# Products of the up-projection and parts of the down-projection by turns in the blocks done in sevens

## The chip, the cores and the metric

The kernel runs on one core of a Trainium2 chip. The metric is the time of one execution on the device in microseconds (us): before the change 2946.87, the median of three runs from 2945.6 to 2947.86.

The core has a matrix engine (TensorE, PE in the rows; its weight loads are PEld), a vector engine (VectorE, DVE), a scalar engine (ScalarE, ACT) and a general one (GpSimd, POOL). Each works through its own instructions in the order in which the program wrote them, and waits at each for what that one needs. SP issues the transfers (DMA), in order too.

## The reference

One layer of a decoder over 2048 prompt tokens and 64 sample tokens. The mixer in its first half stays as it is; the change lies in the MLP behind it, with D_MODEL = 1024 and D_FF = 4096, all in float32:

```python
h1 = layer_norm(ALPHA * h + mix, ln1_g, ln1_b)
up = jnp.square(jax.nn.relu(jnp.einsum('btd,df->btf', h1, w_up)))
ff = jnp.einsum('btf,fd->btd', up, w_down)
h  = layer_norm(ALPHA * h1 + ff, ln2_g, ln2_b)
```

## The kernel before

Each float32 operand is split into a high part (ScalarE copies it to a rounded type: `uph`, `wdh`, `uh`, `xsh`, `xoh`) and a low part (VectorE subtracts: `upl`, `wdl`, `ul`, `xsl`, `xol`). A product of two such operands is three matmuls (`mm3`, line 1786): high by high, high by low, low by high.

The MLP (`mlp_phase`) takes the tokens in three blocks: five token tiles, then six, then six. Blocks 1 and 2 do the up-projection "in sevens" (`block`, line 2062): hidden features f and f+16, two halves of the inner dimension and two halves of the 768 tokens make a 2 by 2 scheme that needs seven products where the plain way needs eight. A **round** of the loop (`up(j)`, line 2069, j from 0 to 15) makes seven **products** (`seven`): each is 12 matmuls of 384 columns. They go into three PSUM banks of a ring of four ("pu"), here called y, x and d: products 1, 3, 5 and 7 add into y, 2 and 4 into x, 6 into d. Between them y and x are read out (`m1`, `m5`, `u2`, slices of the tile `mt`), so the next product on the same bank must wait for that read. `done` turns a sum into the squared ReLU: three instructions of ScalarE, then one of VectorE for the low part `ul`.

`down(bi, fs, tasks)` (line 1917) is the down-projection of the round before, for its two features. It has 12 **parts**: for each half of the output columns and each token tile, 6 matmuls of 512 columns into one of four banks ("pd"), then an addition by VectorE into the token tile's accumulator `acc`. In a round of before all seven products come first, then all 12 parts. A bank is used again four parts later, when its addition is done.

Weights are loaded two features at a time into a ring of four buffers (`raw`): `unit.load` for the up-projection of the next round, `load_down` for the down-projection. `unit.one` to `unit.seven` make and split the seven combinations into four `slots`; one to four were tasks within the parts, five to seven come behind the first three products. `split_down` splits the down weights into four `wslots`, two for each half of the output.

Between two blocks (`last_two`, line 2012) the last two rounds' parts run back to back, and among them the next block's rows are transposed by TensorE into the "pu" banks and combined (`enters`, line 1842): for each of three pairs of token tiles two sets of transposes (`rows`), the combining (`sums`: seven instructions of VectorE, eight of ScalarE, four of GpSimd) and a scaling of the accumulators by ScalarE (`scale`). One of these steps was taken behind every second part. Layer norms of finished blocks and of the rows to come stand in a list `later`; `step()` takes one of them, and stands behind some products and some parts. `finish` (line 2156) ends the last block and is left as it is.

What runs when is set by the order in which these calls are written: each engine gets its instructions in that order.

Of the kernel before, what the change touches and what calls it, by code (L numbers as in the profile page):

```python
# [8 lines left out]
F32 = mybir.dt.float32  # L9
F32R = mybir.dt.float32r  # L10
U8 = mybir.dt.uint8
AF = mybir.ActivationFunctionType
# [1661 lines left out]
def mlp_phase(ctx, tc, em, a, o, z, banks, sch):  # L1674
# [167 lines left out]
    def enters(bi):  # L1842
# [3 lines left out]
        out = []  # L1846
        for mi in range(3):
# [33 lines left out]
            out += [lambda r=rows: r(0), lambda r=rows: r(1), sums, scale]  # L1881
        return out
# [34 lines left out]
    def down(bi, fs, tasks, last=False, todo=()):  # L1917

        acc = accs[bi % 2]
        n = 0  # L1920
        for hf in range(2):
            for mi, (t0, mt) in enumerate(blocks[bi]):
                ps = bank("pd")
                partial(ps, mi, mt, fs, wslots[2 * hf:2 * hf + 2], True, True)
                s = slice(512 * hf, 512 * hf + 512)
                em.tt(acc[mi][0:mt, s], ps[0:mt], acc[mi][0:mt, s], OP.add)
                if todo and n % 2 == 0:
                    todo.pop(0)()
                for x in tasks.get(n, ()):
                    x()  # L1930
                if n % 4 == 0 and not todo:
                    step()
                n += 1
        if last:
            while todo:
                todo.pop(0)()
            lns = []
            for mi, (t0, mt) in enumerate(blocks[bi]):
                def put(t0=t0, mt=mt, t=acc[mi]):
                    em.dma(o["y"][t0:t0 + mt], t[0:mt])  # L1940

                lns.append(layer_norm(acc[mi], mt, put))
            for i in range(len(lns) + 2):
                for j in range(3):
                    if 0 <= i - j < len(lns):
                        later.append(lns[i - j][j])
# [65 lines left out]
    def last_two(bi, fs, gs):  # L2012

        todo = enters(bi + 1)
        n = len(blocks[bi])
        down(bi, fs, {n + 1: [lambda: split_down(gs, (0,))]}, todo=todo)
        down(bi, gs, {0: [lambda: split_down(gs, (1,))], 2: [unit.one], 4: [unit.two], 6: [unit.three], 8: [unit.four]}, last=True, todo=todo)
# [44 lines left out]
    def block(bi):  # L2062
# [6 lines left out]
        def up(j):  # L2069
# [11 lines left out]

            def done(c, f, c0):
                em.act(c, c, AF.Relu)
                squared(c, f, c0)
# [5 lines left out]
            em.act(m5, x, AF.Copy)  # L2090
            unit.six()
            step()
# [3 lines left out]
            if j:  # L2096
                split_down((j - 1, j + 15), (0, 1) if j == 15 else (0,))
            if j == 15:
                load_down(f, g)
            seven(x, "xs", 12, 3)  # L2100
            em.tt(u2, x, u2, OP.add)
            if j < 15:
                unit.load()
            done(u2, g, 0)
            seven(y, "xs", 8, 0)
            em.tt(m5, y, m5, OP.add)
            if 0 < j < 15:
                split_down((j - 1, j + 15), (1,))
            if j < 15:
                load_down(f, g)  # L2110
            if j == 15 and not end:
                unit.load()
            if not j:
                unit.one()
                unit.four()
            done(m5, g, 384)
            seven(d, "xo", 4, 1, True)
            em.tt(m1, d, m1, OP.add)
            if not j:
                unit.two()  # L2120
            done(m1, f, 0)
            if j == 15 and end:
                late(3, f, 0)
                late(0, f, 1)
                late(1, g, 0)
# [3 lines left out]
            if not j:  # L2129
                unit.three()  # L2130
# [3 lines left out]
            step()  # L2134

        for j in range(16):
            up(j)
            if 0 < j < 15:
                down(bi, (j - 1, j + 15), {2: [unit.one], 4: [unit.two], 6: [unit.three], 8: [unit.four]})
# [171 lines left out]
```

## Time and profile before

| | us |
|---|---|
| median of three runs | 2946.87 |
| the profiled execution | 2953.42 |
| its span, first to last instruction | 2951.3 |
| TensorE busy in the span | 2825.0 (96%) |
| VectorE busy | 1985.0 (67%) |
| ScalarE busy | 1208.6 (41%) |
| GpSimd busy | 511.9 (17%) |
| rounds of block 1, from the first product to the last | 500.28 |
| rounds of block 2 | 492.67 |
| way from block 0 to block 1, and from block 1 to block 2 | 46.08, 46.67 |

TensorE is busy nearly all the time, and its matmuls overlap in the records: each is longer than the distance from its start to the next one's start. What a row of matmuls costs is therefore read from starts. Idle time in the rows stands in brackets, with the instruction that ended it.

### The profile page before, as it was taken

How to read it: one execution, taken by the hardware profiler on the slowest of the kernel's cores; microseconds unless marked ns; L12 is line 12 of the kernel's file. 1: busy time of each engine (PE TensorE's matmuls, PEld its weight loads, DVE VectorE, ACT ScalarE, POOL GpSimd, SP SyncE). 2: the span in 40 equal slices, each digit the busy share in tenths (PEclk: the TensorE clock that was granted, in tenths of full speed). 3: DMA queues.
4: the chain of work that ended last, by engine and by line, in shares of the span. 5: the costliest groups of instructions: out<-in, count | busy, mean ns of one | idle time of the engine just before them, and what ended most of it. 6: DMA issues, size and time to landing. Idle time of an engine off the chain costs nothing.

```text
span 2951.3 us, 54436 instructions
## 1 busy us (share of the span) xinstructions
PE 2825.0 (96%) x21918; PEld 2448.9 (83%) x21918; DVE 1985.0 (67%) x3812; ACT 1208.6 (41%) x2576; POOL 511.9 (17%) x505
## 2 busy tenths in 40 slices
PE   8999999999999999898999999899999989999998
PEld 8988877777778778798988888778888877888887
DVE  5876757868787687845455665675677567666566
ACT  5445323443444335233333333534443454443443
POOL 4332111011011013337100000210001021100003
PEclk9999999999999999899999999999999999999999
DMA  7535444524343443457532222123211112221121
GB/s 269 199 106 200 141 144 126 173 95 145 107 158 116 123 143 103 133 167 242 177 114 84 81 79 79 58 90 114 81 63 58 58 72 79 85 80 58 58 85 59
DMA packets 173773, 339.41 MB, mean 115 GB/s; under 512 B 29776, under 2 KB 51536, under 8 KB 173520
## 3 DMA queue, kind: packets, MB, share of 16 engines
q1 hardware_dynamic: 173520, 335.93, 33.6%
q8 instruction: 172, 2.82, 0.4%
q14 instruction: 81, 0.66, 0.1%
HBM read 272.75 MB, written 63.11 MB: 114 GB/s over the span
## 4 chain that ended last, share of the span: by engine, by line
PE 59%; DVE 18%; issue 11%; ACT 8%; POOL 2%; DMA 2%; SPq 0%; DVEq 0%; POOLq 0%; ACTq 0%
PE bank L97 57%; ACT mt L112 2%; DVE rhsb L156 2%; DVE xt L156 2%; DVE mt L156 2%; POOL raw L156 2%; PE bank L108 2%; DVE wdl L156 1%; DVE xt L1005 1%; ACT uh L112 1%; DVE acc L160 1%; DVE ul L156 1%; ACT uph L112 1%; DVE acc L156 1%; DVE upl L156 1%
## 5 line engine op out<-in xcount | busy, mean ns | idle before, releaser
L97 PE MATMUL bank<-wdh,uh 128*128 128x512 f32 (+1 forms) x1064 | 421.1, 396 | 20.2 <-DVE acc L156 18.9
L156 DVE TENSOR_TENSOR acc<-bank,acc 128x512 f32<-128x512 f32 (+1 forms) x532 | 351.5, 684 | 102.9 <-PE bank L97 100.0
L97 PE MATMUL bank<-wdh,ul 128*128 128x512 f32 (+1 forms) x1064 | 417.0, 392 | 0.0
L97 PE MATMUL bank<-wdl,uh 128*128 128x512 f32 (+1 forms) x1064 | 416.9, 392 | 0.0
L97 PE MATMUL bank<-xh,wh 128*128 128x512 f32 (+1 forms) x1040 | 384.0, 369 | 11.3 <-ACT wh L112 8.1
L97 PE MATMUL bank<-xl,wh 128*128 128x512 f32 (+1 forms) x1040 | 380.5, 366 | 0.7 <-DVE xl L156 0.7
L97 PE MATMUL bank<-xh,wl 128*128 128x512 f32 (+1 forms) x1040 | 375.0, 367 | 0.9 <-POOL wl L156 0.8
L97 PE MATMUL bank<-xoh,uph 128*128 128x288 f32 (+1 forms) x896 | 283.0, 316 | 32.9 <-DVE mt L156 27.8
L156 DVE TENSOR_TENSOR upl<-raw,uph 128x512 fp32r<-128x512 f32 x292 | 201.4, 699 | 162.2 <-ACT uph L112 162.1
L97 PE MATMUL bank<-xoh,upl 128*128 128x288 f32 (+1 forms) x896 | 280.4, 313 | 0.0
L97 PE MATMUL bank<-xol,uph 128*128 128x288 f32 (+1 forms) x896 | 280.2, 313 | 0.0
L97 PEld LDWEIGHTS bank<-wdh,uh 128*128 128x128 f32 (+1 forms) x1064 | 197.4, 186 | 75.9 <-DVE acc L156 33.5
L112 ACT ACTIVATE uph<-raw 128x512 fp32r<-128x512 f32 x292 | 174.4, 623 | 205.7 <-DVE raw L156 182.4
L97 PE MATMUL bank<-wh,xh 128*128 128x256 f32 (+1 forms) x816 | 248.0, 304 | 7.9 <-DVE rs L160 7.9
L97 PE MATMUL bank<-wh,xl 128*128 128x256 f32 (+1 forms) x816 | 234.8, 288 | 3.8 <-DVE xl L156 3.8
L97 PEld LDWEIGHTS bank<-wdh,ul 128*128 128x128 f32 (+1 forms) x1064 | 197.1, 185 | 46.6 <-issue 0.2
L97 PE MATMUL bank<-wl,xh 128*128 128x256 f32 (+1 forms) x816 | 234.9, 288 | 0.0
L97 PEld LDWEIGHTS bank<-wdl,uh 128*128 128x128 f32 (+1 forms) x1064 | 197.6, 186 | 43.1 <-issue 0.2
L97 PEld LDWEIGHTS bank<-xh,wh 128*128 128x128 f32 x1040 | 197.5, 190 | 40.9 <-ACT wh L112 8.3
L156 POOL TENSOR_TENSOR raw<-raw 128x512 f32<-128x512 f32 x64 | 89.2, 1394 | 784.6 <-DVE raw L156 410.9
L97 PEld LDWEIGHTS bank<-xl,wh 128*128 128x128 f32 x1040 | 197.5, 190 | 29.6 <-issue 4.6
L97 PEld LDWEIGHTS bank<-xh,wl 128*128 128x128 f32 x1040 | 196.2, 190 | 29.4 <-issue 4.8
(250 smaller groups left out, 5768.9 us busy)
## 6 DMA issues: line engine op xcount, KB each, us to landing
raw<-in_wup SPq DMA_DIRECT2D x96, 512.0 KB, 3.6
raw<-in_wdown SPq DMA_DIRECT2D x96, 512.0 KB, 4.1
wh<-h_w SPq DMA_DIRECT2D x156, 256.0 KB, 2.6
wl<-l_w SPq DMA_DIRECT2D x156, 256.0 KB, 2.9
raww<-in_wout SPq DMA_DIRECT2D x64, 256.0 KB, 2.8
raww<-in_win SPq DMA_DIRECT2D x52, 256.0 KB, 3.3
h_w<-wh SPq DMA_DIRECT2D x52, 256.0 KB, 2.8
l_w<-wl SPq DMA_DIRECT2D x52, 256.0 KB, 2.4
```

Of the source, the lines that this page charges most:

```text
L97: self.nc.tensor.matmul(out, lhsT, rhs, start=start, stop=stop, skip_group_check=skip)
L108: self.nc.tensor.transpose(out, in_, ident)
L112: self.nc.scalar.activation(out, in_, func, **kw)
L156: (self.nc.vector if eng == DVE else self.nc.gpsimd).tensor_tensor(out, a, b, op=op)
L160: self.nc.vector.scalar_tensor_tensor(out, a, s, b, op0=op0, op1=op1)
L1005: nc.vector.transpose(out, in_)
```

## The change

Three things are written in another order; no instruction of the computation is added or left out.

First, in rounds 1 to 14 of blocks 1 and 2 the 12 parts no longer follow the seven products. `groups` makes a list of them, and `go()` issues two: behind products 2, 3, 4, 5, 6 and 7. Rounds 0 and 15 have no parts among their products, as before.

Second, what went with it: the low part `ul` of each `done` is put off (`lows`, `low()`) until the next product has been issued and its sum read; `split_down` is halved, the first output half behind product 5 of the round itself, the second behind product 2 of the next; `unit.one` to `unit.four` come behind products 5, 6, 6 and 7; `load_down` now comes ahead of `unit.load`, behind product 2, and `unit.load` behind product 3. So the two change places in the ring of four buffers. `step()` is called three times in a round, where it was two times, and three more in the parts.

Third, between blocks the steps of `enters` are taken one behind each of three parts in a row, then a pause of three or four parts, and all scalings at the end.

```diff
+        gap = [None] * (len(blocks[bi - 1]) - 2)
+        return [x for steps in out for x in steps + gap][:-len(gap)] + scales
...
+        return [lambda x=(hf, mi, mt): group(*x) for hf in range(2) for mi, (t0, mt) in enumerate(blocks[bi])]
...
+            parts = groups(bi, (j - 1, j + 15)) if 0 < j < 15 else []
+
+            def go():
+                for _ in range(2):
+                    if parts:
+                        parts.pop(0)()
+
+            lows = []
+
             def done(c, f, c0):
                 em.act(c, c, AF.Relu)
-                squared(c, f, c0)
+                em.act(c, c, AF.Square)
+                uh, ul = [t[:, c0:c0 + 384] for t in us[f]]
+                em.act(uh, c, AF.Copy)
+                lows.append(lambda: em.tt(ul, c, uh.bitcast(F32), OP.subtract))
...
             seven(x, "xs", 0, 1, True)
             em.act(m5, x, AF.Copy)
+            if j:
+                split_down((j - 1, j + 15), (1,))
+            load_down(f, g)
             unit.six()
+            go()
             step()
             seven(y, "xs", 4, 2)
             em.act(u2, y, AF.Copy)
             unit.seven()
-            if j:
-                split_down((j - 1, j + 15), (0, 1) if j == 15 else (0,))
-            if j == 15:
-                load_down(f, g)
+            if j < 15 or not end:
+                unit.load()
+            go()
             seven(x, "xs", 12, 3)
             em.tt(u2, x, u2, OP.add)
-            if j < 15:
-                unit.load()
             done(u2, g, 0)
+            go()
+            step()
             seven(y, "xs", 8, 0)
             em.tt(m5, y, m5, OP.add)
-            if 0 < j < 15:
-                split_down((j - 1, j + 15), (1,))
+            low()
             if j < 15:
-                load_down(f, g)
-            if j == 15 and not end:
-                unit.load()
-            if not j:
+                split_down((f, g), (0,))
                 unit.one()
-                unit.four()
             done(m5, g, 384)
+            go()
             seven(d, "xo", 4, 1, True)
             em.tt(m1, d, m1, OP.add)
-            if not j:
+            low()
+            if j < 15:
                 unit.two()
+                unit.four()
             done(m1, f, 0)
+            go()
+            step()
...
-            if 0 < j < 15:
-                down(bi, (j - 1, j + 15), {2: [unit.one], 4: [unit.two], 6: [unit.three], 8: [unit.four]})
```

On TensorE, in round 1 of block 1 behind product 2 (`xs`, `uph`, `upl` are a product's operands; `wdh`, `wdl`, `uh`, `ul` a part's; six rows like the added ones, into bank 63, stand just ahead):

```order
+L97 MATMUL bank_66<-wdh_15656,uh_15665 128x512
+L97 MATMUL bank_66<-wdl_15657,uh_15665 128x512
+L97 MATMUL bank_66<-wdh_15656,ul_15666 128x512
+L97 MATMUL bank_66<-wdh_15658,uh_15734 128x512
+L97 MATMUL bank_66<-wdl_15659,uh_15734 128x512
+L97 MATMUL bank_66<-wdh_15658,ul_15735 128x512
 L97 MATMUL bank_64<-xsh,uph_14569 128x384
 L97 MATMUL bank_64<-xsl,uph_14569 128x384
```

Two parts now stand between product 2 and product 3, which adds into y's bank (64). The same is so behind each later product of the round.

On VectorE, in a middle round of block 2, around product 5, whose sum is read by the row `mt<-bank_64,mt`. Before:

```order
L156 TENSOR_TENSOR mt<-bank_69,mt 128x384
L156 TENSOR_TENSOR ul_15941<-mt,uh_15940 128x384
L156 TENSOR_TENSOR mt<-bank_64,mt 128x384
L156 TENSOR_TENSOR wdl_15661<-raw_14688,wdh_15660 128x512
L156 TENSOR_TENSOR wdl_15663<-raw_14740,wdh_15662 128x512
L156 TENSOR_TENSOR ul_15941<-mt,uh_15940 128x384
L156 TENSOR_TENSOR mt<-bank_70,mt 128x384
```

Now:

```order
L156 TENSOR_TENSOR mt<-bank_69,mt 128x384
L156 TENSOR_TENSOR acc_4_14457<-bank_63,acc_4_14457 128x512
L156 TENSOR_TENSOR acc_5_15653<-bank_66,acc_5_15653 128x512
L156 TENSOR_TENSOR mt<-bank_64,mt 128x384
L156 TENSOR_TENSOR ul_15941<-mt,uh_15940 128x384
L156 TENSOR_TENSOR wdl_15657<-raw_15695,wdh_15656 128x512
L156 TENSOR_TENSOR wdl_15659<-raw_15697,wdh_15658 128x512
L156 TENSOR_TENSOR upl_14566<-raw_14688,uph_14565 128x512
L156 TENSOR_TENSOR raw_14688<-raw_14740,raw_14688 128x512
L156 TENSOR_TENSOR acc_0_14453<-bank_67,acc_0_14453 128x512
L156 TENSOR_TENSOR acc_1_14454<-bank_68,acc_1_14454 128x512
L156 TENSOR_TENSOR mt<-bank_70,mt 128x384
```

The read of product 5's sum has moved ahead of the `ul` that waits for ScalarE, and additions of parts (`acc`) stand between the reads of sums.

On VectorE, at the end of the way from block 0 to block 1, the third `sums` (the rows of `mt` and `xol`). Before:

```order
L156 TENSOR_TENSOR acc_3_14456<-bank_67,acc_3_14456 128x512
L156 TENSOR_TENSOR upl_14572<-raw_14740,uph_14571 128x512
L156 TENSOR_TENSOR acc_4_14457<-bank_68,acc_4_14457 64x512
L156 TENSOR_TENSOR mt<-bank_64,mt 128x512
L156 TENSOR_TENSOR mt<-mt,bank_69 128x512
L156 TENSOR_TENSOR mt<-bank_69,mt 128x512
L156 TENSOR_TENSOR xol<-bank_69,xoh 128x4x128
L156 TENSOR_TENSOR mt<-bank_65,mt 128x512
L156 TENSOR_TENSOR xol<-bank_64,xoh 128x4x128
L156 TENSOR_TENSOR xol<-bank_65,xoh 128x4x128
L156 TENSOR_TENSOR upl_14566<-raw_14740,uph_14565 128x512
```

Now:

```order
L156 TENSOR_TENSOR acc_4_14457<-bank_67,acc_4_14457 64x512
L156 TENSOR_TENSOR mt<-bank_64,mt 128x512
L156 TENSOR_TENSOR mt<-mt,bank_69 128x512
L156 TENSOR_TENSOR mt<-bank_69,mt 128x512
L156 TENSOR_TENSOR xol<-bank_69,xoh 128x4x128
L156 TENSOR_TENSOR mt<-bank_65,mt 128x512
L156 TENSOR_TENSOR xol<-bank_64,xoh 128x4x128
L156 TENSOR_TENSOR xol<-bank_65,xoh 128x4x128
L156 TENSOR_TENSOR upl_14568<-raw_14688,uph_14567 128x512
L156 TENSOR_TENSOR raw_14688<-raw_14740,raw_14688 128x512
L156 TENSOR_TENSOR acc_0_14453<-bank_68,acc_0_14453 128x512
```

The third `sums` stood behind the last part's addition; now five additions of parts, and the two instructions of `unit.two`, stand behind it.

## Rows read from the trace of the kernel before

**Rows 1.** The page, part 1: busy us, share, instructions.
```profile
span 2951.3 us, 54436 instructions
PE 2825.0 (96%) x21918; PEld 2448.9 (83%) x21918; DVE 1985.0 (67%) x3812; ACT 1208.6 (41%) x2576; POOL 511.9 (17%) x505
```

**Rows 2.** TensorE's waits, 1868.87 to 2908.49: us in total, times, longest.
```profile
PE bank L97 <- DVE mt L156: 27.8, 30, 1.9
PE bank L97 <- DVE acc L156: 13.7, 21, 3.1
```

**Rows 3.** Stretches: from:to, length, busy (instructions) PE PEld DVE ACT POOL, clock, DMA.
```profile
1868.87:2369.15 500.28, 479.00 (x2353) 426.83 (x2354) 332.17 (x534) 214.94 (x407) 54.95 (x55) 0.99 0.22 79
2415.82:2908.49 492.67, 471.87 (x2352) 423.63 (x2353) 317.27 (x513) 215.27 (x408) 51.08 (x46) 1.00 0.19 71
1822.79:1868.87 46.08, 36.37 (x170) 28.21 (x169) 31.17 (x50) 21.30 (x36) 13.88 (x12) 0.91 0.07 23
2369.15:2415.82 46.67, 40.60 (x194) 32.98 (x193) 32.07 (x52) 22.37 (x38) 13.93 (x12) 0.96 0.10 39
1868.87:1905.47 36.60, 33.84 (x168) 33.23 (x169) 22.83 (x38) 23.14 (x43) 9.66 (x9) 0.88 0.17 61
2603.02:2618.72 15.70, 15.01 (x85) 14.71 (x84) 7.28 (x13) 8.38 (x16) 1.30 (x1) 1.00 0.22 75
2618.72:2635.09 16.37, 16.37 (x73) 13.53 (x73) 12.34 (x20) 5.32 (x10) 1.30 (x1) 1.00 0.14 57
2171.43:2188.91 17.48, 16.98 (x74) 13.37 (x74) 14.41 (x22) 5.31 (x10) 1.30 (x1) 1.00 0.13 53
```

**Rows 4.** Timeline of TensorE, one round of block 2: start, length; products, then parts.
```profile
2603.02 0.34 PE L97 MATMUL bank<-xoh,uph 128*128 128x384 f32 x1
...
2605.11 0.34 PE L97 MATMUL bank<-xsh,uph 128*128 128x384 f32 x1
...
2607.23 0.34 PE L97 MATMUL bank<-xsh,uph 128*128 128x384 f32 x1
...
2618.72 0.39 PE L97 MATMUL bank<-wdh,uh 128*128 128x512 f32 x1
...
2620.12 0.39 PE L97 MATMUL bank<-wdh,uh 128*128 128x512 f32 x1
...
2621.49 0.39 PE L97 MATMUL bank<-wdh,uh 128*128 128x512 f32 x1
```

**Rows 5.** Timeline of the same round around the wait ahead of product 7.
```profile
2615.36 0.56 DVE L156 TENSOR_TENSOR ul<-mt,uh 128x384 fp32r<-128x384 f32 x1 [1.71 <-ACT uh L112]
...
2615.84 0.55 DVE L156 TENSOR_TENSOR mt<-bank,mt 128x384 f32<-128x384 f32 x1
...
2616.53 0.41 PE L97 MATMUL bank<-xoh,uph 128*128 128x384 f32 x1 [0.69 <-DVE mt L156]
```

**Rows 6.** VectorE by line and shape, one round, 2603.02 to 2635.09: count, busy, mean ns.
```profile
L156 DVE TENSOR_TENSOR acc<-bank,acc 128x512 f32<-128x512 f32 x12 | 7.9, 684 | 1.5 <-PE bank L97 1.3
L156 DVE TENSOR_TENSOR upl<-raw,uph 128x512 fp32r<-128x512 f32 x7 | 5.0, 710 | 6.0 <-ACT uph L112 6.0
```

**Rows 7.** Timeline of the way from block 0 to block 1, VectorE, then TensorE.
```profile
1832.24 0.67 DVE L156 TENSOR_TENSOR mt<-bank,mt 128x512 f32<-128x512 f32 x1
...
1837.89 1.29 DVE L156 TENSOR_TENSOR xol<-bank,xoh 128x512 fp32r<-128x512 f32 x2 [1.18 <-ACT xoh L112]
...
1857.56 0.80 PE L97 MATMUL bank<-wdh,uh 128*128 128x512 f32 x1 [3.23 <-DVE acc L156]
...
1868.87 0.69 PE L97 MATMUL bank<-xoh,uph 128*128 128x384 f32 x1 [4.57 <-DVE xol L156]
```

**Rows 8.** Timeline of TensorE, block 1, product 2 of round 1.
```profile
1890.14 0.44 PE L97 MATMUL bank<-xsh,uph 128*128 128x384 f32 x1 [1.82 <-ACT c L112]
```

**Rows 9.** Timeline of VectorE, block 1, the longest `ul`.
```profile
1885.41 1.65 DVE L156 TENSOR_TENSOR ul<-mt,uh 128x384 fp32r<-128x384 f32 x1
```

**Rows 10.** The page, part 6: DMA issues, KB each, us to landing.
```profile
raw<-in_wup SPq DMA_DIRECT2D x96, 512.0 KB, 3.6
```

More of the change, by code (lines that the diff above doesn't have):

```diff
@@ L1842, in enters @@
     def enters(bi):
-        out = []
+        out, scales = [], []
         for mi in range(3):
@@ L1879, in scale @@
                     em.act(t, t, AF.Copy, scale=ALPHA)
-            out += [lambda r=rows: r(0), lambda r=rows: r(1), sums, scale]
-        return out
+            out.append([lambda r=rows: r(0), lambda r=rows: r(1), sums])
+            scales.append(scale)
+        gap = [None] * (len(blocks[bi - 1]) - 2)
+        return [x for steps in out for x in steps + gap][:-len(gap)] + scales
     def rest():
@@ L1915, in partial, with groups @@
             mm3(ps[0:mt], uh[:, c0:c0 + mt], ul[:, c0:c0 + mt], wh, wl, first and i == 0, last and i == len(fs) - 1)
-    def down(bi, fs, tasks, last=False, todo=()):
+    def groups(bi, fs):
         acc = accs[bi % 2]
[L1920 to L1929, printed above, removed]
-                    x()
[L1931 to L1946, printed above, removed]
@@ new lines, in group, with down @@
+        def group(hf, mi, mt):
+            ps = bank("pd")
+            partial(ps, mi, mt, fs, wslots[2 * hf:2 * hf + 2], True, True)
+            t = acc[mi][0:mt, 512 * hf:512 * hf + 512]
+            em.tt(t, ps[0:mt], t, OP.add)
+        return [lambda x=(hf, mi, mt): group(*x) for hf in range(2) for mi, (t0, mt) in enumerate(blocks[bi])]
+    def down(bi, fs, tasks, todo=()):
+        for n, g in enumerate(groups(bi, fs)):
+            g()
+            if todo:
+                x = todo.pop(0)
+                if x is not None:
+                    x()
+            for x in tasks.get(n, ()):
+                x()
+            if n % 4 == 0 and not todo:
+                step()
@@ L1948, in next_rows, with last_norms, put @@
+    def last_norms(bi):
+        lns = []
+        for mi, (t0, mt) in enumerate(blocks[bi]):
+            def put(t0=t0, mt=mt, t=accs[bi % 2][mi]):
+                em.dma(o["y"][t0:t0 + mt], t[0:mt])
+            lns.append(layer_norm(accs[bi % 2][mi], mt, put))
+        for i in range(len(lns) + 2):
+            for j in range(3):
+                if 0 <= i - j < len(lns):
+                    later.append(lns[i - j][j])
     def next_rows(bi):
@@ L2016, in last_two @@
         down(bi, fs, {n + 1: [lambda: split_down(gs, (0,))]}, todo=todo)
-        down(bi, gs, {0: [lambda: split_down(gs, (1,))], 2: [unit.one], 4: [unit.two], 6: [unit.three], 8: [unit.four]}, last=True, todo=todo)
+        down(bi, gs, {0: [lambda: split_down(gs, (1,))], 2: [unit.one], 4: [unit.two], 6: [unit.three], 8: [unit.four]}, todo=todo)
+        while todo:
+            todo.pop(0)()
+        last_norms(bi)
     class Unit:
@@ L2128, in up @@
                 late(2, g, 1)
-            if not j:
+            low()
+            if j < 15:
                 unit.three()
@@ L2133, in up @@
             squared(c, f, 384)
-            step()
+            go()
         for j in range(16):
             up(j)
-            if 0 < j < 15:
-                down(bi, (j - 1, j + 15), {2: [unit.one], 4: [unit.two], 6: [unit.three], 8: [unit.four]})
             if not end:
```

4 lines of the change are left out of this document (added).

## The prediction

> **What bounds the kernel now.** The page first: TensorE is busy for 2825.0 of 2951.3 us, VectorE for 67%, ScalarE for 41% [rows 1]. So time can only go where TensorE idles or runs slowly. The rounds of blocks 1 and 2, which the change rewrites, are 500.28 + 492.67 = 992.95 us long [rows 3]; TensorE's waits there come next: 27.8 us in 30 waits for a `mt` of VectorE, 13.7 us in 21 waits for an `acc` [rows 2]. The reader is to see that both releasers are VectorE, though VectorE is busy for 7.28 + 12.34 = 19.62 of the 32.07 us of an ordinary round [rows 3]. It is not too slow, it does things in the wrong order.
>
> That shows in one round [rows 5]. Product 7 adds into y and must wait until VectorE has read product 5's sum (`mt`, at 2615.84). VectorE came to it late, because ahead of it in the queue stood the `ul` of the sum before, which idled 1.71 us for ScalarE's three instructions. TensorE had only product 6 to do meanwhile and idled 0.69. The waits for `acc` are in rounds with norms: there the parts take 17.48 instead of 16.37 [rows 3], since steps of norms stand between the additions, and a bank is wanted again four parts later.
>
> **What TensorE must do in a round.** From start to start [rows 4]: a product on `xo` takes 2605.11 - 2603.02 = 2.09, one on `xs` 2607.23 - 2605.11 = 2.12. Three and four of them make 6.27 + 8.48 = 14.75; the round of before took 15.70, so its wait with the slow restart behind it costs 0.95. The parts: the first behind the products takes 2620.12 - 2618.72 = 1.40, the second 1.37, and the ten others (16.37 - 2.77) / 10 = 1.36.
>
> **The change part by part.** *Turns.* Two parts stand behind each of products 2 to 7. A pair behind a product has been seen to take 1.40 + 1.37 = 2.77, so six take 16.62, which is 0.25 dearer than the 12 parts in a row. Bounds: 2.72 if the switch costs nothing, 2.80 if both parts pay for it; with 6 x 28 = 168 pairs that is 8 us less or 5 more. I take 2.77, the row of just this order. A round would be 31.37.
>
> *Do the waits go?* Product 7 now has two pairs and product 6 between it and the sum that it waits for: 2.77 + 2.09 + 2.77 = 7.63 instead of 2.09, and the read stands ahead of the waiting `ul`. The other products on y and x have at least a product and a pair, 4.9 us, for one copy. A bank of the parts is wanted again two products and a pair later, some 6.9 us, where it was three parts, 4.1. What does VectorE do in that time? Its longest stretches stand behind products 5 and 6: a `mt` (0.55), a `ul` (0.56), four splits or differences (about 0.7 each), then two `acc` (0.68 each) [rows 5, 6], in all 5.3 us against a product and a pair of 4.9; behind product 6 one less of them, 4.6, but a step of a norm on top in some rounds. So it falls behind by some 0.4 us and in rounds with norms by perhaps 1.5, and makes it good behind product 7 and product 1, where it has little. GpSimd can stretch it: one `ul` took 1.65 instead of 0.56 [rows 5, 9]; two such in a round are 2.2 more. Sum 3.7, still under the 6.9. The last `ul` of a round is wanted by the next round's first pair, a pair and two products (7.0) after product 7; ScalarE's three take 1.7, its split ahead of them and two operations of VectorE some 2 more. I find no wait of TensorE in rounds 2 to 14, with norms or without, and price it at nothing; what hides it all is 16.6 us of parts, spread. If that cover has a hole, it costs up to the old 0.95 a round.
>
> *The load that is moved.* `unit.load` must wait until `unit.seven` has read the old weights, about 2 us behind product 3. The landing takes 3.6 [rows 10], the second of the two about one more. Its user, `unit.one`, stands behind product 5, two pairs and two products (9.8) after product 3. So 7.8 are left for 4.6. In SP's queue only `load_down` and a norm's store stand ahead of it, and both are let go before. Behind a late landing ScalarE would hold `done`, VectorE the `ul`, and only then TensorE: another 3.5 us.
>
> *The sum for the rounds.* Each block has 16 x 14.75 + 14 x 16.62 = 468.7, both 937.4: 55.6 less than 992.95. Three things stay. Rounds 0 and 1 meet without parts: product 2 of round 1 waits for ScalarE's read of y, 1.82 before [rows 8]; round 0 has now the load's wait in it, 4.6 against two products less 2, but on the other hand the reads go first; I keep 1.9 in each block, 3.8 (bounds 0 and 8). The clock: the first two rounds of block 1 ran at a granted clock of 0.88 [rows 3], part of it at the lower level of 1.2 GHz, behind an idle time of 4.57 [rows 7]; that is 0.12 x 36.60 = 4.4 us, kept (bounds 0 and 9). And the last `ul` of round 15 stands behind the late splits that `finish` waits for: 0.5 (0 to 1.2). In round 15 itself the wait ahead of product 7 goes with the new order of VectorE alone. So the rounds win 55.6 - 8.7 = 46.9.
>
> *The ways between the blocks.* 46.08 and 46.67 us [rows 3]. One `sums` holds VectorE from 1832.24 to 1839.18, 6.9 us [rows 7], and TensorE can run only four parts, 5.5 us, into free banks until it needs an addition that stands behind; that is its wait of 3.23. The change starts the first `sums` two parts sooner, which is worth up to 2.7. The third one moves ahead of five additions and of `unit.two`: TensorE needs 6.9 + 1.4 + 0.7 = 9.0 of VectorE and has 5.5 of parts, so a wait of 3.5 to 6 there takes the place of the 4.57 at the next block's first product. The steps moved bring GpSimd's subtractions and ScalarE's scalings with them; neither stands in front of VectorE. I take nothing for both ways together, with 5 us to either side.
>
> *What a rule says against the change.* The parts of before change their bank every 1.36 us, and their clock is 1.00 throughout [rows 3]. The Trainium skill, page "TensorE: Matmul & The Clock Gate", section "A second HAM failure mode: psum-queue depth-cycling", tells of a kernel whose groups cycle through PSUM banks, idle briefly between groups, and so let the clock swing. By it the turns over seven banks would be suspect; by the row they are not, as long as no idle time stands between groups. It is the third rival below.
>
> **The sum.** 46.9 + 0 = 47 us. The profiled execution took 2953.4 (2951.3 and 2.1 around it) and would take 2906; it stands 6.5 above the median of the runs, of which I take the same 47: 2946.9 - 47 = 2900.
>
> **The rivals.** *A wait in place of the wait.* Every round still stops once, elsewhere, as long as before (0.95), say because VectorE's lag and GpSimd's stretching add up; only the waits of the rounds with norms go. For it: VectorE idles 6.0 us a round for ScalarE's splits alone [rows 6], and in order one late operand delays all. Against it: the margins above of 3 us. It gives 28 x 0.95 = 27 us back: 2927.
>
> *No effect.* The interleaved groups turn out dearer by what the waits cost, for instance 3% on every matmul of the rounds; rows of pairs speak against it. 2947.
>
> *The clock, ending slower.* If the small gaps between groups make the clock swing in the rounds, they lose in proportion: at 0.95 the 937 us grow by 47 and the change is worth nothing, so that is the point from which it decides; at the 0.91 of the way between blocks [rows 3] they grow by 84: 2984. For it: the clock did fall in block 1, behind idle times. Against it: those were of 1.8 to 4.6 us, and the turns leave none.
>
> *The load, ending slower.* If landings of `unit.load` took more than 7.8 + 3.5 = 11.3 us, each further us would cost 28; from 13 on the change loses (at 14: 2975). The 3.6 speaks against it.
>
> **How the numbers follow.** Forecast 0.78; a wait in place of the wait 0.12; no effect 0.04; clock 0.02; load 0.02; the rest a gain above the range. The forecast's own spread is from 2886 (cheap switches, no low clock) to 2920 (dear switches, ways 5 worse, some 0.3 of wait a round); with half of the first rival the range is 2886 to 2923. A measurement tells about 0.2% (6 us) from no change: faster 0.93, same 0.03, slower 0.04.
>
> **What would show it.** In the changed profile the rounds should be 31.4 us long each, the same with norms and without; TensorE's wait for `mt` should be nearly gone, that for `acc` be left only between the blocks; pairs of parts should take 2.77 from start to start; the wait for `c` in round 1 should stay at about 1.9; the clock should be 1.00 in the rounds; both ways should stay near 46. A wait of ScalarE for `in_wup` in every round, a clock under 0.97 in the rounds, or rounds over 32 us would make the prediction wrong.

## The result and the profile after

The changed kernel takes 2897.98 us, the median of 4 runs (2897.06 to 2898.47); the kernel before takes 2947.18 beside it (4 runs, 2945.6 to 2947.86). The ratio is 0.983, with a 95% interval from 0.982 to 0.985: 49.2 us faster. The prediction was 2900 (2886 to 2923). The profiled execution of after took 2897.06, its span is 2895.2.

The page of after, part 1, answers to [rows 1]:
```profile
span 2895.2 us, 54566 instructions
PE 2810.3 (97%) x21918; PEld 2449.6 (85%) x21918; DVE 1982.9 (68%) x3812; ACT 1208.1 (42%) x2576; POOL 511.2 (18%) x505
```
No engine has more or fewer instructions of work. TensorE's busy time fell by 14.7 us and the span by 56.1, so most of what went was idle. Of the 56.1, 7.7 have nothing to do with the change: the way from block 0 to block 1 starts at 1822.79 in the profile of before and at 1815.10 here, behind stages that are the same in both. From there to the end it is 1128.5 before and 1080.1 after, 48.4 less. Where a text below says "by the traces", two profiles were lined up in that way too.

TensorE's waits from the first round of block 1 to the last of block 2 (1859.98 to 2852.33; total, times, longest), to be held against [rows 2]:
```profile
PE bank L97 <- DVE acc L156: 10.4, 3, 4.8
PE bank L97 <- ACT c L112: 3.8, 2, 2.0
```
The 30 waits for a `mt` of VectorE are gone. The three that are left for `acc` lie all in the second way between blocks. The two for `c` are one in round 1 of each block, as before ([rows 8]: 1.82).

Stretches of after (length; busy time and instructions of PE, PEld, DVE, ACT, POOL; granted clock; DMA share; GB/s), to be held against [rows 3]: the rounds of blocks 1 and 2, the two ways, the first stretch of block 1, one round:
```profile
1859.98:2329.64 469.66, 467.88 (x2353) 425.00 (x2352) 332.31 (x534) 213.48 (x406) 52.94 (x53) 1.00 0.23 84
2383.88:2852.33 468.45, 466.45 (x2353) 423.57 (x2352) 312.65 (x507) 212.39 (x404) 47.06 (x43) 1.00 0.20 75
1815.10:1859.98 44.88, 36.27 (x170) 28.11 (x169) 31.37 (x50) 23.47 (x40) 16.38 (x13) 0.92 0.06 24
2329.64:2383.88 54.24, 43.84 (x193) 35.60 (x193) 35.98 (x56) 25.50 (x43) 16.40 (x13) 0.91 0.11 37
1859.98:1882.39 22.41, 20.63 (x110) 20.30 (x108) 17.22 (x28) 14.62 (x28) 4.14 (x6) 0.93 0.13 48
2607.00:2638.19 31.19, 31.19 (x157) 28.16 (x156) 19.45 (x33) 13.69 (x27) 2.59 (x2) 1.00 0.19 68
```
The rounds went from 992.95 to 938.11 us, 54.8 less. In the round of the last line TensorE is busy for the whole 31.19; VectorE's 19.45 are what they were. The first way became 1.2 shorter, the second 7.6 longer. The end, from the last round on, is 42.9 (42.8 before). So 54.8 - 6.4 = 48.4.

The timeline of TensorE in the round, to be held against [rows 4]: the first matmul of product 1 on `xo`, of product 2 on `xs`, of a pair of parts, of product 3 on `xs`, of the next pair, of product 4:
```profile
2619.24 0.34 PE L97 MATMUL bank<-xoh,uph 128*128 128x384 f32 x1
...
2621.33 0.34 PE L97 MATMUL bank<-xsh,uph 128*128 128x384 f32 x1
...
2623.45 0.40 PE L97 MATMUL bank<-wdh,uh 128*128 128x512 f32 x1
...
2626.19 0.34 PE L97 MATMUL bank<-xsh,uph 128*128 128x384 f32 x1
...
2628.28 0.40 PE L97 MATMUL bank<-wdh,uh 128*128 128x512 f32 x1
...
2631.04 0.34 PE L97 MATMUL bank<-xsh,uph 128*128 128x384 f32 x1
```
A product on `xo` still takes 2.09, product 2 still 2.12; but product 3, which now stands behind a pair, takes 2628.28 - 2626.19 = 2.09 like the one on `xo`. A pair takes 2.74 to 2.77 (here 2626.19 - 2623.45 and 2631.04 - 2628.28).

### The profile page after: what moved, and what is told of

Read it like the earlier page. It is cut to its first block, busy times and chain, and to the rows that moved or that the text cites. A ratio compares the mean times of both kernels' runs of the same rounds, so it can differ in the third digit from the quotient of the medians.

```text
span 2895.2 us, 54566 instructions
## 1 busy us (share of the span) xinstructions
PE 2810.3 (97%) x21918; PEld 2449.6 (85%) x21918; DVE 1982.9 (68%) x3812; ACT 1208.1 (42%) x2576; POOL 511.2 (18%) x505
## 4 chain that ended last, share of the span: by engine, by line
PE 79%; DVE 12%; issue 3%; ACT 3%; DMA 2%; POOL 1%; SPq 0%; POOLq 0%; DVEq 0%; ACTq 0%
PE bank L97 77%; PE bank L108 2%; DVE xt L156 2%; DVE rhsb L156 2%; DVE xt L1005 1%; DVE et L160 1%; DVE rs L160 1%; DMA raww<-in_wout 1%; DVE et L900 1%; DVE mt L156 0%; POOL wl L156 0%; DVE bk L160 0%; DVE upl L156 0%; ACT ht L112 0%; ACT xsh L112 0%
## 5 line engine op out<-in xcount | busy, mean ns | idle before, releaser
L156 POOL TENSOR_TENSOR raw<-raw 128x512 f32<-128x512 f32 x64 | 82.8, 1294 | 814.6 <-DVE raw L156 358.4
```

Of the source, the lines that this page charges most:

```text
L156: (self.nc.vector if eng == DVE else self.nc.gpsimd).tensor_tensor(out, a, b, op=op)
```

## What the order does and what the turns do

**The order of VectorE alone.** The first run keeps all parts in a row as before, and only lets `ul` wait until the next product's sum has been read:
```diff
-                squared(c, f, c0)
+                em.act(c, c, AF.Square)
+                uh, ul = [t[:, c0:c0 + 384] for t in us[f]]
+                em.act(uh, c, AF.Copy)
+                lows.append(lambda: em.tt(ul, c, uh.bitcast(F32), OP.subtract))
...
             em.tt(m5, y, m5, OP.add)
+            low()
```
(and `low()` in the same place behind products 6 and 7).

> The kernel before with one thing of the change: the low part ul of each done is put off until the next product has been issued and its sum read, so VectorE reads product 5's sum ahead of the ul that waits for ScalarE. No turns; the parts stay behind the seven products, with the steps of the norms among them. Theory (the wait ahead of product 7 comes from VectorE's order alone): the 27.8 us of waits for mt in the rounds go nearly all, an ordinary round falls from 32.07 to 31.1, the waits for acc in rounds with norms stay at some 14 us, the time is 2947 - 28 = 2919. Rival (only the cover of the parts between the products removes that wait): 2945 to 2947.

It took 2909.81, a ratio of 0.987 (0.986 to 0.988): 38 us less than the kernel before, which took 2947.72 beside it, where the whole change has 49. TensorE's waits in the rounds of block 1 (total, times, longest):
```profile
PE bank L97 <- DVE acc L156: 4.7, 6, 1.3
PE bank L97 <- DVE xol L156: 4.6, 1, 4.6
PE bank L97 <- ACT c L112: 0.8, 1, 0.8
```
Not one wait for a `mt` of VectorE is left, in block 2 neither (one of 0.6 there is for a `mt` of ScalarE, and stood in the kernel before too). What stays is the wait for `acc` of the rounds with norms. The gain is more than the 27.8 us of [rows 2], for the restart behind each wait went too, and the wait for `c` in round 1 halved.

**The steps of the norms out of the parts.** The second run is the first one with the norms' steps behind products 2, 4 and 6, where after has them, and none between the additions:
```diff
-                if n % 4 == 0 and not todo:
+                if n % 4 == 0 and not todo and not bi:
                     step()
...
             done(u2, g, 0)
+            step()
...
             done(m1, f, 0)
+            step()
...
             squared(c, f, 384)
-            step()
```

> As the run with the order alone, and besides the steps of the norms stand behind products 2, 4 and 6, three in a round, and none among the parts of blocks 1 and 2. Still no turns. Theory (both kinds of waits are a matter of what stands where in VectorE's queue, and the turns are one way among several to mend it): the waits for acc in the rounds go as well, all rounds are 31.1 to 31.3, and with the ways between the blocks as before the time is 2947 - 54 = 2893, some 5 under the changed kernel. Rival (the turns are needed for rounds with norms, whose steps now delay the reads of sums): those 15 or so rounds keep 0.5 to 1 us of wait each, 2900 to 2910.

It took 2893.35, 0.982 (0.980 to 0.983). Its rounds in blocks 1 and 2, and its second way:
```profile
1862.62:2331.60 468.98, 467.61 (x2352) 427.10 (x2353) 334.60 (x533) 211.46 (x407) 52.93 (x55) 0.99 0.23 83
2379.40:2846.88 467.48, 465.52 (x2353) 424.68 (x2354) 319.17 (x512) 211.81 (x408) 49.14 (x46) 1.00 0.21 75
2331.60:2379.40 47.80, 41.95 (x193) 34.01 (x192) 32.44 (x52) 22.57 (x39) 13.93 (x12) 0.93 0.15 53
```
The rounds take 936.5 without any turn, 1.7 less than in after: a round of 7 products and 12 parts in a row is 31.10, one with turns 31.19. No wait for `acc` is in them. So this kernel wins all that after wins, without turns, and by the traces another 5.9 us, mostly in the ways, which stand here as before the change (by the medians it is 4.6, where the intervals of the two ratios overlap).

**The turns alone.** The third run is after with `ul` at once, as before:
```diff
-                lows.append(lambda: em.tt(ul, c, uh.bitcast(F32), OP.subtract))
+                em.tt(ul, c, uh.bitcast(F32), OP.subtract)
```

> The changed kernel with one thing taken back: the low part ul stands right behind ScalarE's three instructions again, ahead of the next sum's read. The turns stay. Theory (between product 5's end and product 7 stand now two pairs of parts and a product, 7.6 us, so VectorE's 1.7 us of idling for ScalarE does not reach TensorE): rounds of 31.2, the time of the changed kernel, 2898. Rival (the order does it, the turns nothing): the wait ahead of product 7 is back with some 0.7 to 0.95 in each round, 2918 to 2925.

It took 2904.17, 0.985 (0.984 to 0.987). Besides the wait for `c` there is in block 1:
```profile
PE bank L97 <- DVE mt L156: 1.5, 2, 0.8
```
The two for `mt` are in rounds 0 and 15, which have no parts to turn with; from 1898 to 2310 TensorE waits for nothing. The turns are thus a full cure of the wait ahead of product 7, and so is the order; the change has both, and needs one. It is the order, not the turns, that helps in rounds 0 and 15.

## The ways between the blocks

The waits of after in the second way, on TensorE's timeline, and VectorE's first and last operation of the first `sums` there:
```profile
2343.95 0.50 PE L97 MATMUL bank<-wdh,uh 128*128 128x512 f32 x1 [2.78 <-DVE acc L156]
...
2359.97 0.50 PE L97 MATMUL bank<-wdh,uh 128*128 128x512 f32 x1 [2.78 <-DVE acc L156]
...
2378.04 0.50 PE L97 MATMUL bank<-wdh,uh 128*128 128x512 f32 x1 [4.84 <-DVE acc L156]
```
```profile
2336.36 0.68 DVE L156 TENSOR_TENSOR mt<-bank,mt 128x512 f32<-128x512 f32 x1
...
2342.01 1.29 DVE L156 TENSOR_TENSOR xol<-bank,xoh 128x512 fp32r<-128x512 f32 x2 [1.18 <-ACT xoh L112]
```
Each of the three `sums` holds VectorE for 6.9 us, and TensorE runs out of banks behind each. The waits add up to 10.4 us. In the second way of before TensorE waited less (total, times, longest; kernel before, 2369.15 to 2415.9):
```profile
PE bank L97 <- DVE acc L156: 5.1, 2, 3.1
PE bank L108 <- ACT c L112: 0.5, 1, 0.5
PE bank L97 <- DVE xol L156: 0.5, 1, 0.5
```
That is 6.1 against 10.4; and the clock fell from 0.96 to 0.91, which is 54.24 x 0.09 - 46.67 x 0.04 = 3.0 more. Together 7.3 of the 7.6.

**The old spacing in the new kernel.**
```diff
-            out.append([lambda r=rows: r(0), lambda r=rows: r(1), sums])
-            scales.append(scale)
-        gap = [None] * (len(blocks[bi - 1]) - 2)
-        return [x for steps in out for x in steps + gap][:-len(gap)] + scales
+            out += [lambda r=rows: r(0), lambda r=rows: r(1), sums, scale]
+        return [y for x in out for y in (x, None)]
```

> The changed kernel with the steps of enters taken as before: one behind every second part, the scaling as the fourth step of each set. The rounds are those of the changed kernel. Theory (the ways of 44.88 and 54.24 us after the change, 46.08 and 46.67 before, are set by the spacing of these steps alone): they go back to about 46 and 47, and the time is 2898 - 6 = 2892, or 2893 with a longer stretch of low clock at the start of block 1. Rival (the second way is longer for another reason, such as the loads that changed places in the ring or the norms' steps left over from the rounds): it stays at 54, and the time at 2898.

2895.56, 0.983 (0.981 to 0.984). Its second way:
```profile
2330.72:2378.22 47.50, 41.93 (x194) 34.19 (x193) 31.94 (x51) 21.51 (x37) 13.93 (x12) 0.93 0.12 42
```
That is 6.7 less than in after. The first way is 44.80, unchanged. Block 2 is 2.5 longer: the granted clock of its first 52.8 us is 0.97, where after has 1.00 (1.6 us), and a wait of 0.6 for a `mt` of ScalarE stands there again. By the traces it is 4.0 us less from the first way on. By the medians it is 2.4, and the runs of the two kernels overlap (2893.82 to 2899.92 against 2897.06 to 2898.47). So the new spacing is no gain; that it is a loss of a few us is what the traces of one execution each say.

**The cause of the wait, cut.** This run is after with each `sums` in three steps, behind three parts in a row, so that additions come in between:
```diff
-            out.append([lambda r=rows: r(0), lambda r=rows: r(1), sums])
+            out.append([lambda r=rows: r(0), lambda r=rows: r(1), sums, sums2, sums3])
...
-        gap = [None] * (len(blocks[bi - 1]) - 2)
+        gap = [None] * (len(blocks[bi - 1]) - 4)
```

> The changed kernel with the combining step of enters (sums) cut into three that stand behind three parts in a row (the three sums into xs; then xo's first quarter and xs's last; then xo's two others), so that VectorE does additions of parts between them. Nothing else is changed. Theory (on the ways TensorE waits because one sums holds VectorE 6.9 us in a row while four banks last 5.5 us, and the low clock comes behind those waits): the three waits of some 1.9 to 4.8 us a way shrink to under 1 or go, the clock stays up, the ways fall from 44.9 and 54.2 to about 40 and 43, and the time is 2882 to 2887. Rival (VectorE's amount of work sets the ways, some 37 us of instructions and its waits for ScalarE, so that cutting only moves the waits): 2895 to 2898.

2885.51, 0.978 (0.977 to 0.980). Both ways:
```profile
1810.97:1849.36 38.39, 34.45 (x170) 26.64 (x169) 29.71 (x46) 17.69 (x33) 16.75 (x13) 0.95 0.08 28
2320.80:2364.41 43.61, 40.13 (x193) 32.94 (x193) 34.50 (x53) 22.24 (x40) 17.38 (x13) 0.96 0.14 46
```
6.5 and 10.6 us less than in after. The waits behind the first two `sums` of each way are gone but for 0.2, and one is left behind the last (3.7 and 3.1). So the ways were long because one `sums` held VectorE's queue for so long. Not all of the 17.1 is a gain: seven operations of ScalarE and four of VectorE now fall into block 1 instead of the first way, and TensorE waits there 1.4 us for a `mt` of ScalarE. Block 1 is 471.44, 1.8 more. By the traces 15.3 us remain, of an execution that was 8 us faster than the median of its runs; by the medians it is 12.5.

## How much room the turns leave

**The load of the weights, later.** In after the load stands behind product 3; here it is written behind product 5.
```diff
             unit.seven()
-            if j < 15 or not end:
-                unit.load()
...
             em.tt(m5, y, m5, OP.add)
             low()
+            if j < 15 or not end:
+                unit.load()
```

> The changed kernel with unit.load moved from behind product 3 to behind product 5, just ahead of unit.one, which uses what it loads. The prediction put 7.8 us between issue and use for a landing of 4.6, and another 3.5 of VectorE's and ScalarE's slack before TensorE would feel it. Now nothing is left of the 7.8. Theory (the slack behind ScalarE takes the whole landing): ScalarE waits some 2 to 3 us for in_wup in each round, TensorE not in rounds 2 to 14, round 1's wait for c grows by 2 to 3 in each block: 2898 to 2904. Rival (in queues that run in order a late load goes through to TensorE): 1 us a round or more, 2925 or over.

2899.41, 0.984 (0.982 to 0.986): no change. In most rounds the load is issued at the same moment as in after, 4.83 us behind `load_down` (2625.41 and 2630.24 there, 2627.02 and 2631.84 here): SP waited for the buffer already, and its new place in the program changes nothing. In one round of each block a norm's store came to stand ahead of it. SP's queue there, and ScalarE:
```profile
2533.44 0.93 SPq L177 DMA_DIRECT2D raw<-in_wdown  x2
2546.02 0.34 SPq L177 DMA_DIRECT2D out_y<-acc  x1
2546.46 1.85 SPq L177 DMA_DIRECT2D raw<-in_wup  x2
```
```profile
2551.99 0.63 ACT L112 ACTIVATE uph<-raw 128x512 fp32r<-128x512 f32 x1 [7.24 <-DMA raw<-in_wup]
```
The load is 2546.46 - (2533.44 + 4.83) = 8.2 us late, ScalarE waits 7.24 for it, and TensorE waits for nothing between 2500 and 2840. ScalarE splits the weights 13.7 us behind the moment at which their load is issued otherwise (2551.99 - 2538.27). The prediction gave 11.3 until TensorE would feel it; there is more.

**The load four times over**, into the same tile, each behind the landing of the one before:
```diff
             self.new = load("up", j), load("up", j + 16)
+            for _ in range(3):
+                for raw, f in zip(self.new, (j, j + 16)):
+                    em.dma(raw, a["wup"][f])
```

> The kernel after with both up-projection weights of a round loaded four times over, each copy into the same tile and so behind the landing of the one before: issue to the last landing takes about 4 x 3.9 = 15.6 us instead of 3.9. In the kernel after the first load is issued 7.75 us before ScalarE splits it (2630.24 and 2637.99), the slack the prediction gave as 7.8; behind that it gave TensorE 3.5 more, 11.3 in all. Theory: (15.6 - 11.3) x 28 = +120 us, 3018. By the slack of VectorE behind product 5 that the ten reductions showed (5.5): (15.6 - 13.2) x 28 = +67, 2965. Rival, with no slack behind ScalarE's wait: (15.6 - 7.75) x 28 = +220, 3118. Other rival: TensorE never feels it, 2898.

3027.67, 1.026 (1.024 to 1.028), 81 slower than before and 130 than after. SP's row in one round, then TensorE's waits in block 2, then the stretch of block 2:
```profile
2631.03 13.92 SPq L177 DMA_DIRECT2D raw<-in_wup  x8
```
```profile
PE bank L97 <- DVE acc L156: 32.0, 14, 3.3
```
```profile
2450.96:2986.01 535.05, 489.96 (x2353) 438.25 (x2352) 309.40 (x508) 211.95 (x404) 46.05 (x43) 0.95 0.47 154
```
The total lies near the theory (3018), its parts don't. ScalarE splits the first of the two last loads some 15.8 us behind the first issue (2646.87 and 2631.03 in this round); a wait of 32.0 / 14 = 2.3 in a round puts the room at about 13.5, not 11.3, which fits the 13.7 without a wait above. In each block TensorE also waits once for some 10.6 us, for the `uph` of round 1. The rounds grew by more than 2.3, by 3.7 in the mean of rounds 2 to 14: some 0.3 is the restart, and the rest is a granted clock of 0.95 in the mean of block 2. That the waits alone bring this about isn't shown, for in five rounds of block 1 with waits as long the clock stayed up (stretch, then TensorE's waits in it):
```profile
2144.50:2345.00 200.50, 186.81 (x930) 167.12 (x928) 130.49 (x213) 78.42 (x152) 19.88 (x21) 1.00 0.48 158
PE bank L97 <- DVE acc L156: 12.4, 5, 3.1
```
So the rival "the load" of the prediction decides later than it said; behind that point each wait costs its own length and the restart, and in many rounds slow matmuls too.

**More work for VectorE.** Ten reductions of 512 columns behind product 5 (0.69 each, 7.2 us with the gaps), into an otherwise unused tile of 4 bytes per partition:
```diff
+        fix["dm"] = pool.tile([128, 1], F32, name="dm")
...
+            for _ in range(10):
+                em.sum(fix['dm'], fix['xoh'][:, 0:512].bitcast(F32))
```

> The changed kernel with ten more instructions of VectorE behind product 5 of each round (each a sum over 512 columns into a scratch column that nobody reads), some 6 us. VectorE's share of a round rises from 19.5 to 25.5 of 31.2 us, still under TensorE's. Theory (what counts is how long an addition may stand behind its part: 9.8 us from product 5's end to the first part that wants the bank of the next pair, of which 5.3 are used): about 1 to 1.5 us of wait for acc in each round, ahead of the pair behind product 7, 2930 to 2940. Rival A (an engine with a smaller share than TensorE costs nothing): 2898. Rival B (each us more on VectorE in the round is a us more of time): 28 x 6 = 168, 3066.

2994.62, 1.016 (1.014 to 1.017). TensorE's wait was where the theory had it (block 1):
```profile
PE bank L97 <- DVE acc L156: 21.8, 14, 1.6
PE bank L97 <- DVE upl L156: 5.5, 1, 5.5
```
But 97 us is more than twice of what it said. A round took 33.37; the wait is 1.6 of the 2.2 more, and the restart behind it 0.3. The rest is a slower pace of the matmuls, without any wait: pairs of some 2.80 and products on `xs` of 2.12. Two runs took this apart: the tile alone, and the tile with four reductions (2.9 us).

> The kernel after with one tile of 4 bytes per partition that nothing uses: it moves the tiles uh, ul and c by 32 bytes and no instruction. In the kernel with ten reductions, which had the same tile, rounds without any wait of TensorE would have run slower: products on xs 2.12 instead of 2.09, pairs 2.80 instead of 2.765. Theory: that is the place of uh and ul. Then the same tempo shows here, rounds of 31.19 + 4 x 0.03 + 6 x 0.035 = 31.5, 28 of them are 9 us: about 2907. Rival: it came from what VectorE does at the time, by its load of 25 to 27 us in a round instead of 19.5; then rounds of 31.19 and 2898 here.

> The kernel after with four reductions of 512 columns on VectorE behind product 5 of every round (0.69 us each with 0.03 between, 2.9 in all), and the unused tile as in the run with the tile alone. With ten (7.2 us) TensorE waited 1.7 a round, so its slack there is 7.2 - 1.7 = 5.5. Theory: 2.9 lie inside that slack, no wait of TensorE in rounds 2 to 14; what is added is a few us in rounds 0 and 15, which have no parts, and at the ends of the blocks: 2 to 10 us over the run with the tile alone, so 2900 to 2917. Rival (the ten hit the rounds by their load on VectorE and not by a slack that ran out): in proportion, four tenths of the 97 us: 2937.

The tile alone took 2912.35, 0.989 (0.987 to 0.990): 14 us slower than after with the same instructions in the same order. With four reductions it is 2925.72, 0.993 (0.991 to 0.994). One round of each, from product 2 to product 2 (tile alone; then four; then ten):
```profile
2635.38:2666.91 31.53, 31.53 (x158) 28.28 (x157) 19.46 (x32) 13.72 (x26) 2.59 (x2) 1.00 0.19 67
```
```profile
2647.58:2679.11 31.53, 31.53 (x158) 28.29 (x157) 21.84 (x36) 13.82 (x26) 2.60 (x2) 1.00 0.19 67
```
```profile
2629.29:2662.66 33.37, 31.81 (x158) 28.23 (x158) 26.98 (x45) 13.77 (x27) 2.58 (x2) 1.00 0.22 79
```
The tile alone makes a round 0.34 longer; four reductions add nothing to that. So the slower pace does not come from VectorE's load: the theory on the place of the tiles stands. The slack behind product 5 lies between 2.9 and 7.2 us, by the wait of 1.6 at about 5.5. What four reductions cost over the tile alone, 13 us by the medians and 15.4 by the traces, lies outside rounds 2 to 14: 6.4 in the first two rounds of the blocks, 5.0 in the ways, 4.0 behind the last round. The ten cost 82 over the tile alone, 86 by the traces: 1.84 in each of the rounds 2 to 14 (48), 18 in the first two rounds of the blocks, and 10 each in the second way and behind the last round. The expectation of the ten had left these places out; that of the four named them.

**The pairs one product earlier.**
```diff
             unit.five()
+            go()
             seven(x, "xs", 0, 1, True)
...
             squared(c, f, 384)
-            go()
```

> The kernel after with the pairs behind products 1 to 6 instead of 2 to 7. In the kernel after, the one xs product that follows a product directly (product 2) runs 2.12, the three behind a pair 2.09. Theory: an xs product is quicker behind parts whatever it is; then product 2 runs 2.09 too, product 1 follows product 7 directly, and a round is 31.19 - 0.03 = 31.16, the time 2897, with no new wait (product 3's addition to y has one pair and two products ahead as before; the pair behind product 1 wants the last ul of the round before 2.1 us sooner, which had some 3 us of slack). Rival: that slack is less, and TensorE waits for ul at the start of each round: up to 0.5 x 28 = 14 us more, 2912.

2902.15, 0.985 (0.984 to 0.987): no gain. Rounds 2 to 14 are 31.17, as the theory said; but in round 1 of each block the first pair now waits for `ul`, behind a wait of 0.5 for `uh`, in place of the wait for `c` (block 2):
```profile
2412.55 0.50 PE L97 MATMUL bank<-wdh,ul 128*128 128x512 f32 x1 [1.88 <-DVE ul L156]
```

**What the runs point to.** The last run has no turns: order and steps as in the second run, `sums` cut in three, in the last product of round 0 the read of y ahead of a split, and the waiting `ul` ahead of the late splits:
```diff
             if j == 15 and end:
+                low()
                 late(3, f, 0)
...
             low()
-            if not j:
-                unit.three()
             c = ring("c", 2, [128, 384], F32)
             em.act(c, y, AF.Relu)
+            if not j:
+                unit.three()
```

> The kernel with the order alone and the norms' steps behind products (no turns), with the combining step cut in three as in the other run of this call, the read of y at the end of a round put ahead of unit.three's split on ScalarE in round 0, and the last round's low part put back ahead of the late splits. Theory: from 2893.4 the ways win some 5 each, the read of y some 0.5 a block, the last round 1: about 2882. Rival (turns and cut sums are the better pair, since the parts behind the products leave VectorE less even work): 2885 or more, no better than the changed kernel with cut sums.

2877.34 (2876.07 to 2880.43), 0.976 (0.975 to 0.978), faster than both kernels, and 5 us under what was expected. Block 1's longest wait:
```profile
PE bank L97 <- ACT mt L112: 1.7, 1, 1.7
```
The wait for `c` is gone from round 1; the next late one there, for `mt`, costs nearly as much. The rounds are 468.80 and 465.67, the ways 38.39 and 44.14. By the traces it is 20.6 under after, 16.6 of it in the ways and 3.6 in the rounds. Which of its four edits gave what was not run apart, nor whether turns with the same other edits would do as well.

## Why the prediction was right, step by step

**The time was right, two of its terms were not.** The rounds were to win 46.9 and won 54.8; the ways were to cost nothing and cost 6.4. That the sum, 47 against 48.4, is so close is luck: these two nearly cancel.

*The wait and its cause* were right: VectorE did things in the wrong order. The order alone takes all 30 waits for VectorE's `mt` away. "What hides it all is 16.6 us of parts, spread" was not needed for that.

*Do the waits go?* Yes, at no price in rounds 2 to 14. "I find no wait" rested on 5.3 us of VectorE's work against a lead of 6.9; by the reductions the room that is left behind product 5 is about 5.5, more than the 1.6 that these two leave. The prediction had put the `acc` waits of rounds with norms down to the steps between the additions, and the second run bears that out: with the steps elsewhere they go, without turns. What the prediction left open is that the turns are then not needed.

*The products and parts.* A round was to be 14.75 + 16.62 = 31.37 and is 31.19. The pairs were nearly right: 2.77 was taken, and 2.758 behind a product on `xs` and 2.766 behind one on `xo` are the medians. The products were 0.1 too dear, for a product on `xs` behind a pair runs 2.09 where the row was of one behind a product, 2.12. 28 x 0.18 = 5.0 us of the 7.9.

*Three things stay.* The wait for `c`: 1.9 in each block taken, 1.78 in block 1 and 2.0 in block 2 measured. The low clock at the start of block 1 was kept with 4.4; of after's first stretch 22.41 x 0.07 = 1.6 is left, so the other 2.8 of the 7.9. The wait of 4.57 ahead of the block's first product [rows 7] is not there any more: the prediction moved it into the way and left its price in the rounds. The 0.5 for the end were 0.1.

*The ways* are the mis-sized term: 0 within 5, and 6.4. "A wait of 3.5 to 6 there takes the place of the 4.57": the third `sums` does just that, with 4.84. But the rows were of the first way. In the second one the wait ahead of the first product was 0.50 and not 4.57, so there was little to be replaced; and the start "two parts sooner, worth up to 2.7" was no gain, since each of the first two `sums` got a wait of 2.78. A second row, of the second way, would have shown it. [rows 2] hid it too: its stretch runs over the second way, and 5.1 of its 13.7 us for `acc`, the 3.1 among them, are waits of that way and not of rounds.

*The load*: the room until ScalarE needs the weights was 7.8 and is 7.75 (issued at 2630.24, wanted at 2637.99). TensorE's was 11.3 and is about 13.5 by the fourfold load.

*The rule that spoke against the change*, the Trainium skill's on psum-queue depth-cycling in "TensorE: Matmul & The Clock Gate", speaks of groups with idle time between them. The granted clock was 1.00 in the rounds of after, with another group of banks every 2 to 3 us and no idle time between the groups. So the row of before decided rightly. How much idle time would let the clock fall here the runs don't tell: with a wait of 1.6 in each round (ten reductions) it stayed at 1.00 in rounds 2 to 14, with waits of 2.5 in the mean (fourfold load) it stayed there in five rounds of block 1, and with 2.3 it was 0.95 in the mean of block 2.

*The rivals.* A wait in place of the wait: none in the rounds, one in the ways. No effect: no. The clock and the load stayed away, for the reasons given.

## What to carry to other kernels

When an engine that is far from busy is waited for, look at what stands ahead of the awaited operation in its queue, and try that order by itself before the big engine's work is woven anew: here it gave 38 us, with the norms' steps 54, and the weaving on top gave nothing. A long run of operations on such an engine wants to be cut where others need it in between; cutting `sums` gave 12. And read a row for each place that a term stands for: two ways that look alike had waits of 4.57 and 0.50 at the same spot.

## What was not expected of the hardware

**The pace of matmuls hung on where three sets of tiles lay.** The unused tile of 4 bytes moved `uh`, `ul` and `c` by 32 bytes (`uh0` from 101504 to 101536) and nothing else. The groups that have `uh` or `ul` as an operand became slower, in block 0 too, at a clock of 1.00 and with TensorE busy all the time. Block 0's matmuls of 512 columns, 1500 to 1780 us, after and then the tile alone (count, busy us, mean ns):
```profile
L97 PE MATMUL bank<-wdh,ul 128*128 128x512 f32 x167 | 65.0, 389 | 0.0
```
```profile
L97 PE MATMUL bank<-wdh,ul 128*128 128x512 f32 x172 | 68.0, 395 | 0.0
```
From start to start the median is 227 ns in after and 232 with the tile; all three kernels that have the tile show 232, all others 227. In a round, the pairs went from 2.758 and 2.766 to 2.797 and 2.788 and products on `xs` behind a pair from 2.088 to 2.122, though their own operands had not moved. That is 0.34 in a round and some 4 us in block 0, about the 14 us measured. Which of the three tiles does it and why was not tried.

**A group's pace hung on the group before.** Products on `xs` take 2.12 behind a product, 2.09 behind a pair; product 2 falls from 2.12 to 2.09 when a pair is put ahead of it (the run with the pairs one product earlier). In a row of twelve matmuls the slow ones alternate 174 and 179 ns from start to start, the quick ones keep to 173 or 174. With the tiles moved, a product on `xs` keeps the slow pattern behind a pair too. The runs don't tell why.

**Short waits that come back in every round did not always cost clock.** Waits of 1.6 us in each round left it at 1.00 in rounds 2 to 14 of the run with ten reductions. With the fourfold load, waits of 2.3 in the mean went with 0.95 in block 2, and waits of 2.5 in the mean with 1.00 in five rounds of block 1. So the length of the waits does not decide alone; what else does stays open.
